# A hybrid diffusion layer on one core: hand-written engine and load orders up to the end of the q projection

## The chip, the cores and the metric

The kernel runs on one core of a Trainium2 chip. The metric is the device time in microseconds of one execution. The core has five instruction streams that matter here: PE (matrix products; PEld is its loading of weights), DVE (vector operations), ACT (scalar and activation operations), POOL (a second vector engine) and SP (which only issues transfers). Each stream runs its own instructions in order and waits on semaphores for the others. Matrix products accumulate in PSUM, eight banks, and their results are copied out by DVE or ACT.

## The reference, cut to what matters

One layer for 640 tokens: 512 latent tokens (four tiles of 128) and 128 context tokens (the fifth tile, number 4). The width is 1024.

```python
def _layer(x, cond, rope, ctx_k, ctx_v, ...):
    mod = (jax.nn.silu(cond) @ w_ada + b_ada)[:, None, :]
    sh1, sc1, g1, sh2, sc2, g2 = jnp.split(mod, 6, axis=-1)
    h = _rms(x, norm_mix) * (1 + sc1) + sh1
    mix, k, v = _mixer(h, rope, ctx_k, ctx_v, ...)      # proj = h @ w_in: q, k, v, conv inputs
    x = x + g1 * mix
    h2 = _rms(x, norm_ffn) * (1 + sc2) + sh2
    gate, up = jnp.split(h2 @ w_gate_up, 2, axis=-1)
    x = x + g2 * ((jax.nn.silu(gate) * up) @ w_down)
    return x, k, v
```

Inside the mixer, `q = _rms(q, q_norm)` and the same for k are followed by the rotary positions on latent tokens, attention, a gated short convolution, and an output projection. Everything is float32. The part of the kernel that is changed computes `h` and `h @ w_in[:, :512]`, the q projection, and the tables of cosines and sines times the norms' gains.

## The kernel before, in words

A product of two float32 matrices is made of three products in a faster format (float32r): each operand is split into a rounded high part and a low part, the difference, and `mm3` adds high x high, high x low and low x high. `split` makes the two parts, the high one on ACT (L150), the low one on DVE (L151).

The start works in eight rounds k, one for each 128 rows of the model's width. Before the rounds each of the five tiles of x is loaded, its squares are summed on ACT (L476), its scale is made by DVE and POOL (`rstd_of`, L162 and L164), it is scaled by DVE (L478), turned by PE in eight transposes (L439), and copied from PSUM to `xT` by DVE or ACT (L450, L452). For every k:

- `ada1_mm(k)`, the step "a": a block of `w_ada` of 1 MB, loaded in two halves of two transfers each into a ring `af` of four halves, is multiplied by the condition in 16 products (L379); DVE copies the result (L421).
- `ada1_mod(k)`, the step "m": four small products turn that result (L428); DVE makes scale and shift of block k from it (`mod_evict`, L402 to L406).
- `h_do(k, ...)`, the step "h": the modulated tile, on ACT for the latent tokens (L462) and on DVE for the context (L464), then the split into `hH[k]` and `hL[k]`.
- `q_mm(k, t)`, the step "q" for each token tile t: three products of 512 columns (L154 to L156) into the accumulator of the tile. The weights of q come as four transfers, each for two rounds; a transfer lands in a ring `wf` of three buffers and is split into rings `wh`, `wl` of four.

The order of the work is set in this way. A string of steps, `P1PRE`, is written out for the first round and the work before it; in it the orders of DVE, ACT and POOL are kept as written. The other seven rounds follow the pattern `P1SEQ`, in which only PE's order is kept as written: m and h for block k+1, a for block k+2, then five q products. A planner orders the other engines there from costs and priorities. SP's transfers are ordered by the planner all the way; `LOADS` gives only the order in which the first of them are asked for. Weights are asked for a few places ahead of their use (`W`, `AHEAD`): the two transfers of the k and v weights and the first of the convolution's are asked for within the rounds.

PSUM has two banks of kind t, two of kind c and two pairs of kind s at this stage. The turned tiles 0 to 2 use the pairs, tiles 3 and 4 and the m products use t, the a products use c. The q accumulators take both pairs and one of c when the first q product comes.

At the end of q the five accumulators are copied out (L549, L551). Then the rotary tables are made: two transfers on ACT's queue (L561, L562) and ten POOL operations (L568, L574). Products for k and v follow (PE names them `pc`, 256 columns), then attention, which PE runs from a third written string, `SEQ`.

Of the kernel before, what the change touches and what calls it, by code (L numbers as in the profile page):

```python
# [86 lines left out]
LOADS = [0, 0, 0, 0, 2, 1, -1, 0, 3, 3, 2, 2]  # L87
# [3 lines left out]
def build(ctx, tc, x_prompt, x_sample, c, cache_k, cache_v, c_ctx, norm_mix, norm_ffn, w_ada, b_ada,  # L91
# [144 lines left out]
    def load_split(e, wf):  # L236
# [4 lines left out]
        if gain is None:  # L241
            with early(SOQ[key[1]] if key[0] == 'q' else SOW):
# [109 lines left out]

    for a in LOADS:
        if a > 0:
            ada1_next(a)
        elif a < 0:
            load_next(True)
        else:
            x_load()
# [53 lines left out]
    def ada1_mm(k):  # L413
# [3 lines left out]
        for h, wf in enumerate(ada1[k]):  # L417
            for i in range(4):
                cond_mm(rp, 4 * h + i, wf[:, i].rearrange("p a b -> p (a b)"))
        res = T("res", (P, 256), F32, 2)  # L420
        dve.tensor_copy(res, rp)  # L421
        ada1[k] = res

    def ada1_mod(k):
        res = ada1.pop(k)
        mp = PB((P, 2, 1, 2))
# [5 lines left out]

    def xT_do(t):

        both = PS2() if t < XB else None
        tps = [both[:, i] if t < XB else PB() for i in range(2)]

        def turn(k):
            pe.transpose(tps[k // 4][:, k % 4 * P:(k % 4 + 1) * P], xs[t][:, k * P:(k + 1) * P], ident)  # L439

        if t < XB:
            for k in range(KD):
                turn(k)
        for i, tp in enumerate(tps):
            if t >= XB:
                for k in range(4):
                    turn(4 * i + k)
            dst, src = xT[:, 4 * i:4 * i + 4, t * P:(t + 1) * P], tp.rearrange("p (k q) -> p k q", q=P)
            if XTE[2 * t + i] == 0:
                act.activation(dst, src, AF.Copy)  # L450
            else:
                dve.tensor_copy(dst, src)  # L452
# [3 lines left out]
    def h_do(k, cc):  # L456
# [3 lines left out]
        a, b = modA[0][:, k, cc:cc + 1], modB[0][:, k, cc:cc + 1]  # L460
        if cc == 0:
# [3 lines left out]
        if k == 0:  # L465
# [3 lines left out]

    pe_order = tc.manual_schedule(engines={mybir.EngineType.PE})  # L470
    pe_order.__enter__()

    def x_norm(t):
# [3 lines left out]
        r = rstd_of(ss, 1, 1.0 / D)  # L477
        dve.tensor_scalar_mul(xs[t], xs[t], r)  # L478
# [9 lines left out]
    qacc = []  # L488

    def q_mm(k, t):  # L490
        if not qacc:
            qa, qb = PS2(), PS2()
            qacc.extend([qa[:, 0], qa[:, 1], qb[:, 0], qb[:, 1], PB(tag="c")])
        wh, wl = W(("q", k // 2))
        s = slice(t * P, (t + 1) * P)
        mm3(qacc[t], hH[k][:, s], hL[k][:, s], wh[:, k % 2], wl[:, k % 2], k == 0, k == KD - 1)
# [15 lines left out]
    steps = {"r": x_norm, "c": late_consts, "w": lambda i: load_split(*deferred.pop(0)), "p": lambda i: rows2_load(), "x": xT_do, "v": lambda i: (vec_do, vec2_do)[i](), "m": ada1_mod, "a": ada1_mm}  # L512
    pre_order = tc.manual_schedule(engines={mybir.EngineType.DVE, mybir.EngineType.Activation, mybir.EngineType.Pool})
    pre_order.__enter__()
    in_pre[0] = True
    for x in P1PRE.split():
        k = int(x[1])
        if x[0] == "h":
            h_do(k, int(x[2]))
        elif x[0] == "q":  # L520
            q_mm(k, int(x[2]))
        else:
# [7 lines left out]
    for k in range(1, KD):  # L530
        ada1_next(3)
        for x in P1SEQ.split():
            if x == "m" and k + 1 < KD:
                ada1_mod(k + 1)
            elif x == "h" and k + 1 < KD:
                h_do(k + 1, 0)
                h_do(k + 1, 1)
            elif x == "a" and k + 2 < KD:
                ada1_mm(k + 2)
            elif x.isdigit():  # L540
                q_mm(k, int(x))
        if k == 2:
            vec2_do()

# [18 lines left out]
    gains, tabs = [], []  # L563
    for nm, g in (("q", q_norm), ("k", k_norm)):
        gb_ = gain_rows[nm]
        tab = T("tab", (P, 2, NL, HD), F32, 2)
        cg, sg = tab[:, 0], tab[:, 1]
        pool.tensor_tensor(cg, rc, gb_.unsqueeze(1).to_broadcast([P, NL, HD]), ALU.mult)  # L568
        s4 = sg.rearrange("p t (a b c) -> p t a b c", a=2, b=2)
        r4 = rs_.rearrange("p t (a b c) -> p t a b c", a=2, b=2)  # L570
        g4 = gb_.rearrange("p (a b c) -> p a b c", a=2, b=2)
        for b in range(2):
            for a in range(2):
                pool.tensor_tensor(s4[:, :, a, b], r4[:, :, a, b],  # L574
                                   g4[:, a, 1 - b].unsqueeze(1).to_broadcast([P, NL, 16]), ALU.mult)
        gains.append(gb_)
# [747 lines left out]
```

## Time and profile before

| | |
|---|---|
| median of 3 runs | 760.62 us (759.63 to 762.23) |
| the profiled execution: time | 762.66 us |
| the profiled execution: span of the core | 760.9 us |
| PE busy over the span | 739.5 us (97%) |
| DVE, ACT, POOL busy over the span | 552.7, 369.6, 43.1 us |
| first product behind q (k and v) | starts at 64.82 us |
| mean granted clock of PE | 0.993 |

The profile is of one execution and its times count from the start of the span. The span is a little shorter than the execution's time. PE's share of busy time is high throughout, but a busy PE is not PE at its peak, since its clock can be cut to half. The profile gives the granted clock for any stretch (1.00 is full). In a row of the timeline the first number is the start, the second the length, and the bracket behind it the idle time of the engine before the instruction and what ended it.

### The profile page before, as it was taken

How to read it: one execution, taken by the hardware profiler on the slowest of the kernel's cores; microseconds unless marked ns; L12 is line 12 of the kernel's file. 1: busy time of each engine (PE TensorE's matmuls, PEld its weight loads, DVE VectorE, ACT ScalarE, POOL GpSimd, SP SyncE). 2: the span in 40 equal slices, each digit the busy share in tenths (PEclk: the TensorE clock that was granted, in tenths of full speed). 3: DMA queues.
4: the chain of work that ended last, by engine and by line, in shares of the span. 5: the costliest groups of instructions: out<-in, count | busy, mean ns of one | idle time of the engine just before them, and what ended most of it. 6: DMA issues, size and time to landing. Idle time of an engine off the chain costs nothing.

```text
span 760.9 us, 11844 instructions
## 1 busy us (share of the span) xinstructions
PE 739.5 (97%) x4580; PEld 664.6 (87%) x4580; DVE 552.7 (73%) x1003; ACT 369.6 (49%) x715; POOL 43.1 (6%) x73
## 2 busy tenths in 40 slices
PE   4999999999999999999999999999999999999997
PEld 3768888989998887899898789998889998899986
DVE  5556987676666797779879678884578866788653
ACT  5345867666656444765552135553125541255410
POOL 3104301011010110100000000000000000000000
PEclk9899999999999999999999999999999999999999
DMA  9985132522433363031335223223113132222312
GB/s 289 293 233 158 38 118 91 173 91 91 160 104 93 130 249 111 1 112 56 86 111 179 83 62 103 79 89 113 53 56 110 58 112 67 73 86 82 111 56 84
DMA packets 102349, 84.52 MB, mean 111 GB/s; under 512 B 4526, under 2 KB 82674, under 8 KB 102292
## 3 DMA queue, kind: packets, MB, share of 16 engines
q1 hardware_dynamic: 100980, 83.39, 35.5%
q8 instruction: 36, 0.59, 0.3%
q10 hardware_dynamic: 1056, 0.26, 0.2%
q0 software_dynamic: 256, 0.11, 0.1%
q14 instruction: 21, 0.17, 0.1%
HBM read 79.68 MB, written 2.75 MB: 108 GB/s over the span
## 4 chain that ended last, share of the span: by engine, by line
PE 82%; DVE 8%; DMA 3%; ACT 2%; SPq 2%; issue 1%; POOL 1%; DVEq 0%; POOLq 0%
PE pf L154 17%; PE pf L156 16%; PE pf L155 16%; PE pc L677 3%; PE pc L678 3%; PE pc L679 3%; PE po L834 3%; PE ps L791 2%; PE ph L154 2%; PE pt L817 2%; PE ph L155 2%; PE ph L156 2%; PE pc L379 2%; DMA af<-in_w_ada_dram 2%; DMA wf<-in_w_gate_up_dram 1%
## 5 line engine op out<-in xcount | busy, mean ns | idle before, releaser
L150 ACT ACTIVATE wh<-wf 128x1024 fp32r<-128x1024 f32 (+1 forms) x76 | 64.1, 843 | 95.7 <-PE pf L156 61.8
L154 PE MATMUL pf<-wh,gT 128*128 128x512 f32 (+1 forms) x225 | 88.1, 392 | 0.0
L155 PE MATMUL pf<-wl,gT 128*128 128x512 f32 (+1 forms) x225 | 87.7, 390 | 0.0
L156 PE MATMUL pf<-wh,gT 128*128 128x512 f32 (+1 forms) x225 | 87.7, 390 | 0.0
L151 DVE TENSOR_TENSOR wl<-wf,wh 128x1024 fp32r<-128x1024 f32 (+1 forms) x42 | 49.4, 1175 | 29.1 <-ACT wh L150 26.3
L677 PE MATMUL pc<-hH,wh 128*128 128x320 f32 x192 | 61.1, 318 | 0.0
L678 PE MATMUL pc<-hL,wh 128*128 128x320 f32 x192 | 59.4, 310 | 0.0
L679 PE MATMUL pc<-hH,wl 128*128 128x320 f32 x192 | 59.4, 309 | 0.0
L155 PEld LDWEIGHTS pf<-wl,gT 128*128 128x128 f32 x225 | 42.2, 188 | 10.0 <-issue 0.2
L154 PEld LDWEIGHTS pf<-wh,gT 128*128 128x128 f32 x225 | 42.2, 188 | 9.9 <-ACT wh L150 0.2
L156 PEld LDWEIGHTS pf<-wh,gT 128*128 128x128 f32 x225 | 42.2, 188 | 9.8
L154 PE MATMUL pf<-T,wh 128*128 128x320 f32 x160 | 49.7, 311 | 0.5 <-ACT u L1154 0.5
L155 PE MATMUL pf<-T,wl 128*128 128x320 f32 x160 | 49.5, 309 | 0.0
L155 PE MATMUL pf<-T,wh 128*128 128x320 f32 x160 | 49.5, 309 | 0.0
L156 PE MATMUL pf<-T,wh 128*128 128x320 f32 x160 | 49.5, 309 | 0.0
L154 PE MATMUL pf<-T,wl 128*128 128x320 f32 x160 | 49.5, 309 | 0.0
L156 PE MATMUL pf<-T,wl 128*128 128x320 f32 x160 | 49.5, 309 | 0.0
L154 PE MATMUL pf<-B,wl 128*128 128x320 f32 x152 | 47.3, 311 | 0.1
L156 PE MATMUL pf<-B,wl 128*128 128x320 f32 x152 | 47.1, 310 | 0.0
L155 PE MATMUL pf<-B,wl 128*128 128x320 f32 x152 | 47.0, 309 | 0.0
L1233 DVE TENSOR_TENSOR dm<-pf,g 128x512 f32<-128x512 f32 (+1 forms) x41 | 27.7, 675 | 22.8 <-PE pf L156 22.6
L154 PE MATMUL pf<-B,wh 128*128 128x320 f32 x136 | 42.3, 311 | 1.5 <-DVE cu L1183 1.5
(293 smaller groups left out, 2023.9 us busy)
## 6 DMA issues: line engine op xcount, KB each, us to landing
wf<-in_w_gate_up_dram SPq DMA_DIRECT2D x44, 512.0 KB, 4.0
aw<-in_w_ada_dram SPq DMA_DIRECT2D x24, 512.0 KB, 4.7
wf<-in_w_down_dram SPq DMA_DIRECT2D x20, 512.0 KB, 3.4
wf<-in_w_in_dram SPq DMA_DIRECT2D x18, 512.0 KB, 6.1
af<-in_w_ada_dram SPq DMA_DIRECT2D x32, 256.0 KB, 6.0
x<-in_x_sample_dram SPq DMA_DIRECT2D x8, 512.0 KB, 4.8
wf<-in_w_out_dram SPq DMA_DIRECT2D x8, 512.0 KB, 3.9
wf<-in_w_ada_dram SPq DMA_DIRECT2D x8, 512.0 KB, 3.7
```

The costliest lines, as they stand in the source:

```text
L150: act.activation(hi, src, AF.Copy)
L151: dve.tensor_tensor(lo, src, f32(hi), ALU.subtract)
L154: pe.matmul(out, lh, rh, start=start, stop=False, skip_group_check=more)
L155: pe.matmul(out, lh, rl, start=False, stop=False, skip_group_check=more)
L156: pe.matmul(out, ll, rh, start=False, stop=stop, skip_group_check=more)
L379: pe.matmul(out[CG * g:CG * (g + 1)], cp[:, k], w, start=(k < 4), stop=(k >= KD - 4), skip_group_check=True)
L677: pe.matmul(acc, wh[:, k], hH[k][:, c0:c0 + n], start=(k == 0), stop=False)
L678: pe.matmul(acc, wh[:, k], hL[k][:, c0:c0 + n], start=False, stop=False)
L679: pe.matmul(acc, wl[:, k], hH[k][:, c0:c0 + n], start=False, stop=(k == KD - 1))
L791: pe.matmul(s2[:, g, :320], q, kk[:, v, P + g * 320:P + (g + 1) * 320], start=(i == 0), stop=(i == 1))
L834: pe.matmul(ov, w, x[:, i].rearrange("p a q -> p (a q)"), start=(g == 0 and i == 0 and n == 0), stop=(last and i == len(kts) - 1 and n == 1))
L1233: dve.tensor_tensor(dm, ps[:, :n], g2[cc][:, oc], ALU.mult)
```

## The change

It replaces the order of everything up to the end of q. One string, `P1SEQ`, now names every step of the start and of all eight rounds, and the orders of PE, DVE, ACT, POOL and SP are all kept as it is written. The steps are cut finer: scaling a tile ("s") apart from its norm ("r"), each copy of a turned tile ("e", with the engine, d for DVE and a for ACT) apart from its turning ("x"), the copy of an a product ("b") apart from the product, and the two halves of a weight split ("w" on ACT, "l" on DVE) apart. New steps are "d", a number of small products on the identity that go to the fifth accumulator before it is used, "n", the low part of the first modulated tile, and "R", the rotary tables.

- In the rounds, a of block k+2 stands behind two q products of round k instead of ahead of all five; m and h of block k+1 stand at the end of the round before.
- The loads: `LOADS` gives the whole order: all tiles of x, blocks 0 to 7 with q0, q1 and q2 between them, and then q3, the two transfers of k and v weights, and the first of the convolution's. The transfers of the caches come behind that list.
- The first modulated tile (block 0, latent tokens; the step `h00y`): ACT writes the rounded `hH[0]` straight from `xT`, DVE makes the unrounded one beside it, and "n" takes the difference. Before, ACT made the unrounded one, then the rounded one from it.
- Both copies of turned tiles 0 and 1 are DVE's; before, one of each was ACT's.
- The rotary tables are made in round four, from transfers on POOL's queue, in a buffer that is otherwise used late.
- The fifth q accumulator is taken at the start, so the a products and the first two m products share one bank of kind c.

```diff
-SOQ = [0, -300, -300, -300]
-P1SEQ = 'm h a 0 1 2 3 4'
-P1PRE = ('r0 r1 r2 x0 r3 x1 v0 x2 a0 w0 x3 m0 r4 h00 a1 q02 q01 x4 q00 m1 h01 h10 a2 q03 h11 p0 q04 c0')
+P1SEQ = ('d8 r0 s0 x0 r1 s1 r2 e00d x1 s2 e01d r3 v0 d4 x2 s3 e20a a0 e10d b0 e11d e21d x3 m0 d4 w e30a h00y l n0 '
+         'r4 q01 e31d s4 p0 q02 a1 x4 b1 e40d m1 h01x h10 q00 a2 b2 h11 q04 m2 w e41a q03 l q10 h20 q11 q12 h21 a3 b3 q13 q14 '
+         'm3 h30 h31 q20 q21 a4 b4 q22 q23 c0 q24 v1 m4 h40 h41 R q30 q31 a5 b5 w l q32 q33 q34 '
+         'm5 h50 h51 q40 q41 a6 b6 q42 q43 q44 m6 h60 h61 q50 q51 a7 b7 w l q52 q53 q54 '
+         'm7 h70 h71 q60 q61 w l q62 q63 q64 w l w l q70 q71 q72 q73 q74')
-XTE = [0, 1, 0, 1, 1, 1, 0, 1, 1, 0]
-LOADS = [0, 0, 0, 0, 2, 1, -1, 0, 3, 3, 2, 2]
+LOADS = 'xxxxAWxAAWAAWAAAWWWW'
...
+    pe_order = tc.manual_schedule(engines={mybir.EngineType.PE})
+    pe_order.__enter__()
+    pre_order = tc.manual_schedule(engines={mybir.EngineType.DVE, mybir.EngineType.Activation, mybir.EngineType.Pool,
+                                            mybir.EngineType.SP})
+    pre_order.__enter__()
...
-        mp = PB((P, 2, 1, 2))
+        mp = PB((P, 2, 1, 2), tag="c" if k < 2 else "t")
...
+        if alone and cc == 0:
+            act.activation(hH[k][:, s], xT[:, k, s], AF.Identity, bias=b, scale=a)
+            dve.tensor_scalar(hF[k][:, s], xT[:, k, s], a, b, ALU.mult, ALU.add)
+            return
...
-    qacc = []
+    qacc = [PB(tag="c")]
...
+    def spin(n):
+        for _ in range(n):
+            pe.matmul(qacc[-1][:, :P], ident, ident, start=True, stop=True)
...
+    def w_hi(_):
+        e, wf = deferred.pop(0)
+        a, b = e[1].shape[1], e[1].shape[2]
+        e[5] = T("wh", (P, a, b), F32R, WHB), T("wl", (P, a, b), F32R, WHB)
+        act.activation(e[5][0], wf, AF.Copy)
+        rounded.append((wf, *e[5]))
...
+    def rope_tables():
+        rt = T("oz", (P, 2, NL, HD))
+        rc, rs_ = rt[:, 0], rt[:, 1]
+        pool.dma_start(rc, rope_c.rearrange("(t p) d -> p t d", p=P))
+        pool.dma_start(rs_, rope_s.rearrange("(t p) d -> p t d", p=P))
...
-    for k in range(1, KD):
-        ada1_next(3)
-        for x in P1SEQ.split():
...
-    rt = T("pr", (P, 2, NL, HD), F32, PRB)
-    rc, rs_ = rt[:, 0], rt[:, 1]
-    act.dma_start(rc, rope_c.rearrange("(t p) d -> p t d", p=P))
-    act.dma_start(rs_, rope_s.rearrange("(t p) d -> p t d", p=P))
```

More of the change, by code (lines that the diff above doesn't have):

```diff
@@ L241, in load_split @@
         if gain is None:
[L242 removed]
+            with early(SOW):
                 split(wh, wl, wf)
@@ L556, in build @@
     open_psum("pp2", {"t": PT, "c": 5 - PT, "o": 1, "s": 1})
-    rt = T("pr", (P, 2, NL, HD), F32, PRB)
-    rc, rs_ = rt[:, 0], rt[:, 1]
-    act.dma_start(rc, rope_c.rearrange("(t p) d -> p t d", p=P))
-    act.dma_start(rs_, rope_s.rearrange("(t p) d -> p t d", p=P))
[L563 to L576, printed above, removed]
-        tabs.append((cg, sg))
     def head_norm(ps, nh, t, which):
```

103 lines of the change are left out of this document (58 added, 45 removed).

## The prediction

> **What bounds the kernel now.** I read the page first, for the clock, then a table of busy time cut where the clock changes, then the timeline of the stretch that the change touches. The page says where to look:
>
> ```profile
> span 760.9 us, 11844 instructions
> PEclk9899999999999999999999999999999999999999
> ```
>
> The profiled execution took 762.66 us, 1.76 more than its span and 2.04 more than the median of 760.62; the sum below is made inside its span and its difference is then taken from the median. After the first tenth the clock never leaves 9, and PE is the bound there. Everything edited lies ahead of the end of q. That start, cut at the clock's changes (columns: stretch, PE, PEld, DVE, ACT, POOL busy, granted clock, DMA share, GB/s):
>
> ```profile
> 14.66:18.07 3.41, 1.18 (x14) 0.71 (x12) 3.07 (x9) 2.57 (x5) 0.23 (x1) 1.00 1.15 298
> 18.07:21.49 3.42, 2.33 (x15) 1.07 (x12) 1.87 (x3) 1.18 (x2) 3.31 (x6) 0.50 1.17 290
> 21.49:24.90 3.41, 3.41 (x14) 2.91 (x13) 0.62 (x1) 0.00 (x0) 0.00 (x0) 0.50 1.16 282
> 24.90:38.56 13.66, 13.66 (x100) 9.98 (x99) 7.70 (x25) 6.50 (x10) 0.00 (x0) 1.00 1.02 297
> 38.56:41.97 3.41, 1.89 (x22) 1.00 (x21) 2.52 (x6) 2.73 (x3) 0.00 (x0) 1.00 1.01 269
> 41.97:45.38 3.41, 3.41 (x14) 2.48 (x8) 1.65 (x4) 1.32 (x2) 0.00 (x0) 0.50 1.09 307
> 45.38:64.82 19.44, 19.44 (x113) 15.13 (x112) 9.05 (x21) 7.25 (x10) 1.42 (x2) 1.00 0.74 207
> ```
>
> The half-clock stretches are 6.83 and 3.41 us long, and each follows 3.41 us in which PE worked 1.18 or 1.89: the clock is judged about every 3.4 us by the share of busy time. DMA is full until 45, and PE has no idle time in 24.90 to 38.56 or from 41.97 on. So the start is bound in turn by loads, by the idle PE's halved clock, and by PE. The PE rows that carry it (start, length, and in brackets the idle time before):
>
> ```profile
> 15.98 0.61 PE L428 MATMUL pt<-sel,res 128*128 128x2 f32 x4 [1.17 <-ACT xT L450]
> 17.64 0.72 PE L379 MATMUL pc<-af,cp 128*32 128x256 f32 x8 [1.06 <-DMA af<-in_w_ada_dram]
> 19.45 1.08 PE L379 MATMUL pc<-af,cp 128*32 128x256 f32 x8 [1.09 <-DMA af<-in_w_ada_dram]
> 29.96 0.50 PE L154 MATMUL ps<-wh,hH 128*128 128x512 f32 x1
> 41.57 0.75 PE L379 MATMUL pc<-af,cp 128*32 128x256 f32 x8 [1.52 <-DMA af<-in_w_ada_dram]
> 52.74 1.07 PE L379 MATMUL pc<-af,cp 128*32 128x256 f32 x16
> 53.74 0.50 PE L154 MATMUL ps<-wh,hH 128*128 128x512 f32 x1
> 57.35 0.50 PE L428 MATMUL pt<-sel,res 128*128 128x2 f32 x4
> 57.71 0.48 PE L154 MATMUL ps<-wh,hH 128*128 128x512 f32 x1
> 64.82 0.28 PE L154 MATMUL pc<-wh,hH 128*128 128x256 f32 x1
> ```
>
> q of round one begins at 29.96, and q ends at 64.82, where the k and v product starts. Between starts, a modulation product (a) costs 53.74 - 52.74 = 1.00, a q round 57.35 - 53.74 = 3.61, an m 0.36. Two stalls stand out: three waits of 1.06 to 1.17 before 19.45, and one of 1.52 before 41.57.
>
> **The change, part by part.** *The order of the loads.* These are SP's issues before:
>
> ```profile
> 30.71 1.31 SPq L224 DMA_DIRECT2D wf<-in_w_in_dram  x2
> 32.12 4.97 SPq L323 DMA_DIRECT2D af<-in_w_ada_dram  x4
> 37.19 2.48 SPq L224 DMA_DIRECT2D wf<-in_w_in_dram  x1
> 39.76 5.62 SPq L323 DMA_DIRECT2D af<-in_w_ada_dram  x6
> 2.00:28.00 26.00, 17.08 (x111) 12.48 (x112) 13.27 (x36) 11.85 (x22) 7.03 (x13) 0.87 1.07 313
> 28.00:48.00 20.00, 18.48 (x121) 13.36 (x124) 10.53 (x29) 9.41 (x11) 0.00 (x0) 0.91 1.03 288
> ```
>
> The half block that PE awaited at 41.57 was issued behind two q weights (30.71). Changed, q3 and the kv weights stand behind all modulation blocks. By 28.00 some 313 x 26 = 8.14 MB have come, which covers the five x tiles (2.62), blocks 0 to 3 (4.19), q0 and q1 (1.05) and the small rows (0.13). At 288 GB/s block 4 (1.05 MB) then ends near 31, q2 (0.52) near 33, and blocks 5, 6, 7 near 36.6, 40.3 and 43.9. The semaphore comes later than the bytes: before, the awaited half stood at 11.2 MB (x, blocks 0 to 5, four q weights, caches and rows), that is 38.6 by this sum, and came at 41.57; the second half of block 1 stood at 5.3 MB, 18.9 by 313 GB/s, and came at 19.45. So I add 0.5 to 3 us. PE will want blocks 3 to 7 near 29.5, 34, 39, 44 and 49 (worked out below), since each a now stands behind two q products; block 3 (bytes near 27.5) is the only one close. I take the stall as gone: 1.52 saved, and the halved clock after it (3.41 at 0.50 is 1.7 of work; I count 1.6). If the later bound of the lag holds, block 3 costs up to 1.5.
>
> Wait that is added: DVE's b (the copy of a product) stands in a written order, so a late block holds the weight splits and h tiles queued behind it. They are used a round later, about 5 us, which covers it; without the cover q waits as long as the block. Blocks k+2 still wait for a of block k, as before, since the ring is unchanged.
>
> *The first round and the spins.* The rows they are made from (the last is four f32 products of 512 columns):
>
> ```profile
> 9.87 0.60 ACT L450 ACTIVATE xT<-ps 128x512 f32<-128x512 f32 x1 [0.57 <-PE ps L439]
> 10.19 0.75 DVE L478 TENSOR_SCALAR x<-x,rs 128x1024 f32<-128x1024 f32 x1 [0.66 <-POOL rs L164]
> 10.86 0.68 DVE L452 COPY xT<-ps 128x512 f32<-128x512 f32 x1
> 11.60 1.09 PE L439 MATMUL ps<-ident,x 128*128 128x128 f32 x8
> 12.62 1.16 PE L379 MATMUL pc<-af,cp 128*32 128x256 f32 x16
> 15.56 1.22 DVE L151 TENSOR_TENSOR wl<-wf,wh 128x1024 fp32r<-128x1024 f32 x1
> 17.29 0.15 DVE L402 TENSOR_TENSOR modt<-pt,vec 128x2 f32<-128x2 f32 x1
> 17.80 0.81 ACT L462 ACTIVATE hF<-xT,modB,modA 128x512 f32<-128x512 f32 x1 [0.84 <-DVE ms L162]
> 18.65 0.63 ACT L150 ACTIVATE hH<-hF 128x512 fp32r<-128x512 f32 x1
> 19.31 0.69 DVE L151 TENSOR_TENSOR hL<-hF,hH 128x512 fp32r<-128x512 f32 x1
> 20.59 0.42 DVE L421 COPY res<-pc 128x256 f32<-128x256 f32 x1 [0.59 <-PE pc L379]
> 26.47 0.34 DVE L464 TENSOR_SCALAR hF<-xT,modA,modB 128x128 f32<-128x128 f32 x1
> 129.62 1.72 PE pc L739 x4
> ```
>
> The spins, sixteen small products on the identity: 1.72 / 16 is 0.11 for 128 columns, 0.22 cold, so the first eight take 0.9 to 1.8 while x0 is still being loaded and scaled, and four take 0.4 to 0.9 in each of two gaps. Cost 0; at worst 0.5 where x2 is ready sooner than worked out here. They hold the fifth accumulator from the start, so a1 must wait for m0's eviction (done long before its data) and a2 for m1's.
>
> x0's two copies are now both DVE's, with a scaling between: 9.87 + 0.68 + 0.75 + 0.68 is 12.0, so x2 starts near 12.1 instead of 11.60 and a0 near 13.2 instead of 12.62: 0.5 lost. But m0's eviction now comes behind three copies and b only: b0 (0.42) ends near 14.7, e11 and e21 near 16.1, so the eviction (three operations like the one of 0.15, some 0.5) runs at 16.1 to 16.6 where it began at 17.29. Rounding directly, hH of tile 0 is there 0.81 later (17.5; before it took 0.81 + 0.63 and ended at 19.3). The low part gains less: DVE's own scale and add (128x512; between 0.34 and 0.75, I take 0.45), the weight's low part (1.22) and the difference (0.69) give 19.0 against 20.0. So two q products run in the gap before block 1's second half (19.45) and end near 20.0 at full clock. Then a1 ends at 21.0, x4 (1.09) at 22.1, its copy 0.68 and m1's eviction end at 23.4; h01 and h10 (0.34, then 0.81 on ACT) at 24.9; then 0.34 on DVE, a rounding on ACT and a difference, each 128x640 (0.7 to 0.8 by the 128x512 rows), end at 26.9. PE meanwhile does q00, a2, q04, m2, q03 and can begin q10 near 26.4.
>
> But the clock: between 14.66 and 18.07 PE now does half of x3 (0.6), m0 (0.4), four spins (0.4 to 0.5) and one q product (0.2), about 1.7 of 3.41, less than the 1.89 that cost the clock at 41.97. So 18.07 to 21.49 is slow again; after 18.8 PE is then kept busy, and I take the second slow stretch (21.49 to 24.90) as gone. That delays q10 by about 1.0, to 27.4. The Trainium skill, "TensorE: Matmul & The Clock Gate", section on HAM oscillation, asks only that no gap exceed about 3.4 us. Here a gap of 1.52 was enough, so the trace disagrees; by the rule q10 would stay at 26.4.
>
> *Tables, cache loads, splits.* One POOL row and the DVE row behind it:
>
> ```profile
> 66.36 2.15 POOL L574 TENSOR_TENSOR tab<-pr,gnk 128x64 f32<-128x64 f32 x4
> 68.23 0.28 DVE L586 TENSOR_REDUCE hq_ss<-ph 128x2 f32<-128x128 f32 x1 [0.75 <-ACT ph L584]
> ```
>
> The rotary tables' ten POOL operations and two loads leave the end of q for round four, where POOL has nothing; loads go from ACT's queue to POOL's, behind the five gain rows that are there already. Before, POOL ended them at 68.51 and DVE's first user waited for ACT, not for POOL: gain 0, at most the 0.75 shown. Without the move they would now be late, so it keeps the gain rather than makes one. The caches' loads go behind SP's written list, whose last entry waits for q3's split, which stands behind a7 (49) in the order, near 51; with the lag above they land ahead of 57, before q ends. The late constants and the second row of vectors move inside the start and are first used behind q: 0. The split of conv0's weights stays ahead of q's last round, covered by q. From q's end the same PE order follows, moved as a whole: 0, between -0.7 and +1.5, since another order on DVE and ACT behind q could cost a wait.
>
> **Sum.** Round one starts 29.96 - 27.4 = 2.56 sooner, less a3 (1.00), which before stood ahead of it; plus the stall 1.52; plus the clock 1.6: 4.7. q ends near 60.1 and the run takes 760.62 - 4.7 = 755.9 us. With the bounds (block 3 up to 1.5 late, -0.7 to +1.5 behind q, the start 0.7 either way, and not every loss at once) this case spans 754.5 to 758.1.
>
> **Rivals.** *No slow clock at the start* (0.24): the spins and q01 lift the busy share enough; 4.7 + 1.0, so 754.9. This is what the rule of the Trainium skill's page on TensorE named above would give. For it: 1.7 against 1.89 is a near thing. Against it: 2.33 of 3.42 in slow state did not bring the clock back.
>
> *The order does not bring the blocks sooner* (0.09): the ring, not the weights, held them back, and one stall with its slow stretch stays: 4.7 - 1.52 - 1.6 = 1.6 gained, 759.0. For it: DMA is full whatever the order. Against: 0.52 MB fewer stand ahead of block 5.
>
> *Nothing is carried past q* (0.07): attention's start waits for something that did not move, the cache loads or a new order on DVE; the 4.7 is given back, 760.6. Against: before, PE still worked without a break at 64.82.
>
> *Starved rounds, slower* (0.07): a3 to a7 each wait, since each is released to load block k+2 later than before; every stall costs 1.52 and its slow stretch 1.6. From two stalls the gain is gone; with three the run is 3 x 3.1 - 4.7 = 4.6 slower, 765.2. It decides once blocks 4 to 7 and q2 (4.7 MB in the 19.5 us from 29.5 to 49) come at under 241 GB/s. Against: 288 was seen.
>
> **How the numbers follow.** The forecast has 0.53. A measurement can tell about 0.3%, 2.3 us, from no change. Forecast and warm start are faster (0.77), the next two the same (0.16), starvation slower (0.07). The range 752.5 to 759.5 takes in the first three cases: at its low end the warm start with 1.4 of gains from the bounds and 1.0 for the spread of runs (759.63 to 762.23 before), at its high end the third case. It leaves out the last two.
>
> **What would show it.** Right: q's end near 60; no idle PE above 0.7 us after q10; q10 near 27; one half-clock stretch ahead of 25 and none near 42; hH of tile 0 ending near 17.5; tables done by 50. Wrong: PE idle in front of L379 in several rounds (starved), an unchanged first use of round one (the first round's chain misjudged), or q ending at 60 with the later PE rows not moved (nothing carried).

## The result: slower by 0.3%, and the profile after

| | before | after |
|---|---|---|
| median | 760.38 us (759.62 to 762.23, 14 runs) | 762.75 us (761.23 to 764.56, 14 runs) |
| ratio after to before | | 1.003, 95% interval 1.0021 to 1.0039 |
| profiled execution: time, span | 762.66, 760.9 us | 763.84, 762.1 us |
| first k and v product (q's end) | 64.82 us | 63.09 us |
| from there to the first score product of attention | 12.61 us | 14.91 us |

The changed kernel is slower, by about 2.4 us. In its profiled execution q ends 1.73 us sooner, but the stretch behind q is 2.30 longer. The timeline of PE of the changed kernel (start, length, and in brackets the idle time before and what ended it; a0, the first modulation product, is the first row):

```profile
12.73 1.07 PE L385 MATMUL pc<-af,cp 128*32 128x256 f32 x16
15.03 1.14 PE L507 MATMUL pc<-ident 128*128 128x128 f32 x8
16.83 0.50 PE L155 MATMUL ps<-wh,hH 128*128 128x512 f32 x1 [0.67 <-ACT hH L470]
25.55 0.39 PE L155 MATMUL ps<-wh,hH 128*128 128x512 f32 x1
28.25 0.64 PE L385 MATMUL pc<-af,cp 128*32 128x256 f32 x8 [0.19 <-issue]
31.25 1.08 PE L385 MATMUL pc<-af,cp 128*32 128x256 f32 x8 [2.37 <-DMA af<-in_w_ada_dram]
63.09 0.28 PE L155 MATMUL pc<-wh,hH 128*128 128x256 f32 x1
70.58 0.37 PE L647 MATMUL pt<-identr,osq 128*128 128x128 f32 x2 [1.64 <-ACT osq L639]
```

The first q product runs at 16.83 and round one (q10) begins at 25.55, 4.41 ahead of the 29.96 of before and 1.85 ahead of the forecast. Then two waits stand out: 2.37 us for the second half of block 3, where the forecast allowed up to 1.5, and 1.64 behind q, for ACT, where it has nothing. The table of busy time, cut at these places (columns as in the prediction):

```profile
17.00:24.77 7.77, 7.31 (x60) 4.45 (x61) 5.56 (x14) 2.09 (x5) 5.08 (x8) 1.00 1.14 305
24.77:28.25 3.48, 3.29 (x15) 2.11 (x14) 2.52 (x6) 2.95 (x5) 0.00 (x0) 1.00 1.15 269
28.25:31.25 3.00, 0.64 (x8) 0.18 (x9) 0.82 (x1) 0.41 (x1) 1.82 (x5) 0.96 1.17 288
31.25:34.66 3.41, 3.41 (x14) 2.18 (x15) 0.42 (x1) 0.00 (x0) 2.05 (x6) 0.53 1.04 301
34.66:63.09 28.43, 28.43 (x178) 20.60 (x176) 15.85 (x39) 14.24 (x20) 0.00 (x0) 1.00 0.75 226
69.00:78.00 9.00, 6.18 (x41) 5.90 (x41) 6.79 (x26) 4.98 (x15) 3.46 (x4) 0.81 0.25 72
```

The granted clock is full (1.00) up to 31. Each of the two waits is followed by about 3.4 us at half clock: 0.53 in 31.25 to 34.66, and 0.81 in the mean of 69 to 78. Between 34.66 and 63.09 PE is busy all the time. What held block 3 back is seen in the issues, SP's first and then POOL's, of the same execution:

```profile
18.18 0.83 SPq L225 DMA_DIRECT2D wf<-in_w_in_dram  x1
19.05 0.47 SPq L589 DMA_DIRECT2D ck<-in_cache_k_dram  x1
19.57 0.43 SPq L591 DMA_DIRECT2D cv<-in_cache_v_dram  x1
20.13 9.74 SPq L324 DMA_DIRECT2D af<-in_w_ada_dram  x8
...
21.91 0.79 POOL L555 DMA_DIRECT2D oz<-rope_c_dram  x1
22.69 0.78 POOL L556 DMA_DIRECT2D oz<-rope_s_dram  x1
```

The caches are asked for at 19.05, not behind SP's list: their two issues (L589, L591) stand behind the end of the written part, and the planner put them ahead of block 3. The rotary tables' transfers go out at 21.91, not in round four: POOL's queue had nothing to wait for. Together 0.39 MB stand ahead of or beside block 3 where the DMA engines are full (share 1.14 to 1.17 above). And q1, the issue at 18.18, stands ahead of block 3 as well, 0.52 MB more. In the kernel before it was the other way round. These are SP's issues there; the first row ends with the four transfers of block 3, and the last is q1:

```profile
17.29 4.55 SPq L323 DMA_DIRECT2D af<-in_w_ada_dram  x5
21.89 0.83 SPq L527 DMA_DIRECT2D ck<-in_cache_k_dram  x1
22.77 0.43 SPq L529 DMA_DIRECT2D cv<-in_cache_v_dram  x1
23.24 0.43 SPq L224 DMA_DIRECT2D wf<-in_w_in_dram  x1
```

The chain of waits of the changed kernel has both losses (start, length, what):

```profile
22.05 9.07 DMA af<-in_w_ada_dram
...
58.14 1.05 ACT wh L526
59.21 1.24 DVE wl L533
60.47 4.98 DMA wf<-in_w_in_dram
65.53 1.07 ACT wh L151
```

The last transfer of block 3 took 9.07 us from issue to landing. Behind q the chain is another one: ACT and DVE split the k and v weights only at 58.14 and 59.21, behind m7 and h7 in the written order. That frees the buffer for the convolution's second load at 60.47, which lands near 65.5. Its split then stands on ACT in front of the k norm (L610) for which PE waits.

### The profile page after: what moved, and what is told of

Read it like the earlier page. It is cut to its first block, busy times and chain, and to the rows that moved or that the text cites. A ratio compares the mean times of both kernels' runs of the same rounds, so it can differ in the third digit from the quotient of the medians.

```text
span 762.1 us, 11916 instructions
## 1 busy us (share of the span) xinstructions
PE 742.6 (97%) x4612; PEld 666.7 (87%) x4612; DVE 553.9 (73%) x1005; ACT 368.0 (48%) x713; POOL 43.8 (6%) x75
## 4 chain that ended last, share of the span: by engine, by line
PE 84%; DVE 6%; DMA 5%; ACT 2%; issue 1%; SPq 0%; POOL 0%; DVEq 0%; ACTq 0%
PE pf L157 17%; PE pf L156 17%; PE pf L155 17%; PE pc L703 3%; PE pc L705 3%; PE pc L704 3%; PE po L860 2%; PE ps L817 2%; PE pc L385 2%; PE ph L155 2%; PE ph L157 2%; PE ph L156 2%; PE pt L843 2%; DMA af<-in_w_ada_dram 2%; DMA es<-t 1%
## 5 line engine op out<-in xcount | busy, mean ns | idle before, releaser
L151 ACT ACTIVATE wh<-wf 128x512 fp32r<-128x512 f32 (+1 forms) x69 | 56.6, 821 | 85.6 <-PE pf L157 62.0
L152 DVE TENSOR_TENSOR wl<-wf,wh 128x1024 fp32r<-128x1024 f32 (+1 forms) x35 | 40.6, 1161 | 28.7 <-ACT wh L151 23.6
```

The source lines that it names most:

```text
L151: act.activation(hi, src, AF.Copy)
L152: dve.tensor_tensor(lo, src, f32(hi), ALU.subtract)
```

## The experiments

Behind each ratio is its 95% interval. q's end is the start of the first k and v product in the profile. "Behind" is the time from there to the first score product, and "half clock" how long the granted clock was 0.5 in the profiled execution. It comes in stretches of 3.4 us, and the place of each stands with it. Before and after, as profiled above, had 10.2 (three stretches) and 6.8. A profile shows one execution, which can lie off the median of its kernel: that of splits_early took 759.66 us, that of small_late 759.46 and that of before_spins 763.91.

| kernel | median us | ratio to before | q's end | behind | half clock |
|---|---|---|---|---|---|
| before_again | 760.67 (1 run) | | 61.32 | 13.03 | 6.8 (20, 74) |
| before_third | 759.16 (1 run) | | 61.56 | 12.62 | 3.4 (19) |
| after_again | 762.55 | 1.0026 (1.0013 to 1.004) | 61.69 | 13.53 | 0 |
| after_third | 761.85 (1 run) | | 61.20 | 13.56 | 6.8 (10, 75) |
| spins_out | 762.35 | 1.0022 (1.001 to 1.0035) | 61.37 | 15.25 | 6.8 (20, 71) |
| first_tile_undone | 762.09 | 1.0026 (1.0011 to 1.0041) | 60.83 | 14.84 | 3.4 (70) |
| tables_late | 761.71 | 1.0008 (0.9995 to 1.0022) | 60.55 | 14.96 | 3.4 (69) |
| small_late | 760.82 | 1.001 (0.9996 to 1.0023) | 60.17 | 13.68 | 0 |
| block3_first | 762.98 | 1.004 (1.0024 to 1.0056) | 62.54 | 13.38 | 3.4 (10) |
| splits_early | 762.2 | 1.0024 (1.0009 to 1.0039) | 60.83 | 12.61 | 3.4 (9) |
| two | 760.63 | 1.0002 (0.9989 to 1.0016) | 59.86 | 12.61 | 3.4 (72) |
| three | 760.04 | 0.9997 (0.9985 to 1.001) | 60.80 | 12.61 | 0 |
| two_a_first | 759.79 | 0.9986 (0.9977 to 0.9996) | 59.66 | 12.61 | 0 |
| before_spins | 761.51 | 1.0019 (1.0006 to 1.0031) | 61.59 | 16.49 | 6.8 (69) |
| before_tables | 762.7 | 1.0027 (1.0012 to 1.0041) | 63.23 | 12.68 | 3.4 (21) |
| spins_tables | 762.57 | 1.0028 (1.0015 to 1.0041) | 62.57 | 12.67 | 6.8 (9) |
| tables_at_22 | 761.39 | 1.0017 (1.0003 to 1.003) | 63.55 | 12.67 | 3.4 (19) |
| spins_tables_at_22 | 762.3 | 1.0036 (1.0021 to 1.005) | 62.61 | 12.68 | 0 |

**Was the execution that the prediction costed an ordinary one?** before_again and before_third are the kernel before, once more each.

> The kernel before, profiled once more. Theory A (the prediction took one slow execution for the rule: 762.66 against a median of 760.4): q ends 1.5 to 2.5 us ahead of 64.8, because the wait of 1.52 on block 5 or a half-clock stretch is shorter or absent, and the stretch from q's end to the context scores (12.6 us) stays. Theory B (the profiled execution is typical): q ends within 0.5 us of 64.8 with the same two stalls.

> The kernel before once more, for its profile. If the profiled execution of the prediction (q's end 64.82, a wait of 1.52 on block 5 and a half-clock stretch at 42) was a rare one, q ends at 61 to 62 here, the waits after 25 are below 0.7 and no half clock lies between 25 and 60. If it was an ordinary one, q ends at 64 to 65 with that wait.

PE's rows of before_third:

```profile
29.07 0.50 PE L154 MATMUL ps<-wh,hH 128*128 128x512 f32 x1
39.78 0.64 PE L379 MATMUL pc<-af,cp 128*32 128x256 f32 x8 [0.62 <-DMA af<-in_w_ada_dram]
61.56 0.28 PE L154 MATMUL pc<-wh,hH 128*128 128x256 f32 x1
67.80 0.36 PE L621 MATMUL pt<-identr,osq 128*128 128x128 f32 x2 [0.38 <-ACT osq L613]
```

It was not. Block 5 was awaited for 0.62 here and 0.56 in before_again, not 1.52; no half clock follows it, and q ends at 61.3 to 61.6, not at 64.82. Among 28 runs of before the mean granted clock was 0.9958, and only 4 had the 0.993 of the costed execution or less.

**Do the two losses of the change recur?** after_again and after_third are the changed kernel.

> The changed kernel, profiled once more and timed beside the variants. Theory A (the loss is behind q): from q's end to the first context scores it takes 14 to 15 us again, against 12.6 before, with PE idle 1.2 to 2.2 us ahead of the first turned keys; q's end moves between runs with block 3's landing (60 to 63). Theory B (the loss is in the start): the stretch behind q is 12.6 to 13 in this profile and q ends later than 62.5. The time is 762.0 to 763.5 beside variants of 762.2 (splits earlier) and 760.8 (small transfers later).

> The changed kernel once more, for its profile. Theory (two losses that belong to its order): PE waits 1.3 to 2.4 for the second half of block 3 near 30, 1.3 to 2.2 for ACT behind q, and the stretch from q's end to the scores takes 13.5 to 15.3 where 12.6 is had with the splits early. Rival (the losses are chance of the executions seen): one of the two waits is below 0.6.

Block 3 was awaited for 1.38 and 0.33 (2.37 at first), and the wait for ACT behind q was 1.31 and 1.33 (1.64 at first). So the wait behind q recurs, and the one on block 3 varies: where the start itself was later (a0 at 14.57 in after_third, 12.73 at first), block 3 is nearly in time. q10 began at 26.79 and 27.35, against 28.87 and 29.07 in the two further executions of before.

**Parts undone.** spins_out takes the three groups of small products out of the changed kernel.

```diff
-P1SEQ = ('d8 r0 s0 x0 ... v0 d4 x2 ... m0 d4 w ...
+P1SEQ = ('r0 s0 x0 ... v0 x2 ... m0 w ...
```

> The changed kernel without its sixteen spins. Theory A (the spins keep the clock up): in the changed kernel no stretch ahead of 31 us is at half clock and q of round one starts at 24.8. Without the spins x0 and x1 are turned at half clock (0.22 a transpose instead of 0.14), 18 to 21.5 us is at half clock, and q10 starts 1 to 2.5 us later; but block 3 lands at the same 31.3, so q ends within 0.5 us of 63.1 and the time stays within 0.1%. Theory B (the early start comes from the written order alone): q10 stays within 0.5 of 24.8. Theory C (the spins are worth time to the end): the run is 1 to 2 us slower.

The ratio is 1.0022, within the interval of after. The half clock came back in the first round (20 to 24), a1 began at 20.50 (19.43 in after), and block 3 was no longer awaited: what the start lost was time in which the loads caught up. q10 began at 28.08, and q still ended at 61.37. The clock is the spins' doing: in all six profiles of kernels without them a stretch at half clock begins between 18 and 22, and in none of the 14 with them does one begin between 11 and 31 (in four of those it comes earlier, near 10).

first_tile_undone lets ACT write the unrounded first tile and round it from there, as before.

```diff
-            act.activation(hH[k][:, s], xT[:, k, s], AF.Identity, bias=b, scale=a)
-            dve.tensor_scalar(hF[k][:, s], xT[:, k, s], a, b, ALU.mult, ALU.add)
+            act.activation(hF[k][:, s], xT[:, k, s], AF.Identity, bias=b, scale=a)
+            act.activation(hH[k][:, s], hF[k][:, s], AF.Copy)
```

> The changed kernel with the first modulated tile made as before: ACT writes the unrounded tile and then the rounded one from it. Theory A (it shortens one link of a chain that then waits for block 1 and block 3): hH of that tile comes 0.6 us later, q01 starts 0.6 later, block 3 lands at the same time, the time stays within 0.5 us of 762.6. Theory B (the link is on the path to q's end): the time is 0.6 us or more above.

PE then waits 1.28 for the first tile instead of about 0.65, and block 3 is not awaited at all. The ratio stays: the direct rounding shortens this wait, and nothing of it is left in the time. That it is given back at block 3 is argued only, since block 3 was nearly in time in after_third too, where a0 was as late.

tables_late puts the tables' two transfers on SP behind block 7; small_late puts the two cache transfers there as well.

```diff
-LOADS = 'xxxxAWxAAWAAWAAAWWWW'
+LOADS = 'xxxxAWxAAWAAWAAATWWWW'   # T: rope_c, rope_s (small_late: and the caches), on SP
-        pool.dma_start(rc, ...)
-        pool.dma_start(rs_, ...)
```

> The changed kernel with the rotary tables' two transfers alone (0.26 MB) on SP's queue behind block 7. Theory A (they land beside block 3 since POOL's queue waits for nothing ahead of them, and delay it by 0.26 MB / 0.293 = 0.9 us): the wait on block 3 shrinks by about 0.9, the time is 0.7 to 1.5 us below the changed kernel's 762.6. Theory B (the caches were the larger part): the time stays within 0.4 of 762.6.

> The changed kernel with the transfers of the rotary tables (0.26 MB) and of the caches (0.13 MB) issued on SP's queue behind modulation block 7 instead of beside block 3. Theory A (block 3's second half comes late by the bytes ahead of it): it lands 0.39 MB / 0.293 = 1.3 us sooner, near 29.9, the wait of 2.4 on PE shrinks to about 1.1 and q ends 1 to 1.5 sooner (more where the half-clock stretch behind it goes too: up to 3). Theory B (the ring or the issue holds block 3 back): the wait stays within 0.3 of 2.4. Either way the stall behind q is unchanged, since conv weights still come late.

Both go down, to 1.0008 and 1.001. In small_late block 3 is not awaited and q ends at 60.17; the wait behind q (1.45) stays. So by the medians the transfers' place was worth 1 to 2 us. The intervals don't tell the two kernels apart, and they overlap with that of after_again.

block3_first asks for block 3 ahead of q1 and moves q1's split to the end of round one.

```diff
-... 'm2 w e41a q03 l q10 h20 q11 q12 h21 a3 b3 q13 q14 '   LOADS = 'xxxxAWxAAWAAWAAAWWWW'
+... 'm2 e41a q03 q10 h20 q11 q12 h21 a3 b3 q13 q14 w l '   LOADS = 'xxxxAWxAAAWAWAAAWWWW'
```

> The changed kernel with block 3 asked for ahead of q1, and q1's split moved behind q14. Theory A (bytes ahead): block 3's second half lands 0.52 MB / 0.293 = 1.8 us sooner, near 29.5, q ends 1.5 to 3.5 us sooner, if q1 (then landing near 31) is split before q20 wants it. Theory B (ring or issue): the wait on PE stays at 2.4 and q ends where it did or later. A gain at q's end is cut behind q if conv1's weights still land near 65.5: then the time moves by less than 0.5 us.

The wait on block 3 is down to 0.50, but the next step waits 0.75 for q1's split, and the ratio is 1.004. So here the order only chose which load was late.

splits_early moves one of the two late splits ahead of m7.

```diff
-... q52 q53 q54 ' 'm7 h70 h71 q60 q61 w l q62 q63 q64 w l w l q70 ...
+... q52 q53 q54 w l ' 'm7 h70 h71 q60 q61 w l q62 q63 q64 w l q70 ...
```

> The changed kernel with the split of the first k and v weights written ahead of m7 instead of behind q61, the later ones one place earlier each. Theory A (the stall behind q comes from conv1's weights, whose buffer is freed by that split, and whose own split stands on ACT ahead of the k norm): conv1 lands 2 to 4 us sooner, the 1.64 us of idle PE at 70.6 falls to 0.4 as before, the half-clock stretch of 72 to 75.3 goes, and the run is 2 to 3 us faster (760). Theory B (the stall comes from the norm chain itself now that q ends sooner): the idle PE stays at 1.2 or more and the time stays within 0.5 us.

ACT's rows of splits_early, then PE's row behind q:

```profile
61.03 1.06 ACT L151 ACTIVATE wh<-wf 128x1024 fp32r<-128x1024 f32 x1 [1.65 <-PE pc L157]
62.00 2.04 ACT L598 ACTIVATE of<-ps 128x512 f32<-128x512 f32 x4
...
67.06 0.36 PE L647 MATMUL pt<-identr,osq 128*128 128x128 f32 x2 [0.39 <-ACT osq L639]
```

The convolution's split now runs at 61.03, ahead of q's copies, where it began at 65.53 in after. PE's wait is 0.39, and the stretch behind q is 12.61, as before. All four kernels with this split moved have 12.61, and all eight profiles of the changed kernel without it, parts undone or not, have 13.38 to 15.25. That the late splits lengthen the stretch is shown: by 0.9 us without half clock (after_again), and by 2.3 with it (after). The time does not follow: 2 to 3 us were expected, and the ratio is 1.0024. The profile is of an execution 2.5 us below its median, and what the others lose is not seen.

**Parts put together.** two is small_late and splits_early, three adds block3_first, and two_a_first is two with a5, a6 and a7 directly behind m, ahead of the q products.

```diff
-... m4 h40 h41 R q30 q31 a5 b5 w l q32 q33 q34 ' 'm5 h50 h51 q40 q41 a6 b6 q42 ...
+... m4 a5 h40 h41 b5 R w l q30 q31 q32 q33 q34 ' 'm5 a6 h50 h51 b6 q40 q41 q42 ...
```

> The changed kernel with two edits: transfers of tables and caches behind block 7, and the split of the first k and v weights ahead of m7; block 3 stays behind q1. Theory A (the variant with three edits drew its 760.0 from these two, since block 3 ahead of q1 alone gave nothing): 759.3 to 760.6, no wait on PE above 0.8 us between 24 and q's end, 12.6 us from there to the context scores. Theory B (block 3's place is needed too): a wait of 0.5 to 1.5 on block 3 stays and the time is 760.5 to 762.

> The changed kernel with three edits together: transfers of tables and caches behind block 7, block 3 ahead of q1, the split of the first k and v weights ahead of m7. Theory A (the gain of the start is real, and is lost to block 3's lateness and to the late splits): no wait on PE above 0.8 us between 24 and the end of q, q ends near 59.5 to 60.5, 12.6 us from there to the context scores, and the time is 757.0 to 759.0, faster than before by 0.2 to 0.4%. Theory B (nothing but the order of the first round counts, and it costs as much as it gives): the time stays at 760.5 to 762.

> The two edits, and the modulation products of blocks 5 to 7 put directly behind m again, as before the change, instead of behind two q products. Theory A (each product between q's costs 0.1 to 0.2 us at its borders, and blocks 5 to 7 land in time): a round falls from 5.14 to about 5.0 us, q ends 0.3 to 0.5 sooner, the time moves 0 to 0.5 us down. Theory B (the place behind two q products is what hides the blocks): PE waits 0.5 us or more on blocks 5, 6 or 7 and the time is 0.5 to 2 us up.

All three have 12.61 behind q, and two and three are level with before; for three 757.0 to 759.0 had been expected. The scores begin at 72.47 in two and at 73.41 in three, where the two further executions of before have 74.18 and 74.35. So the start's gain reaches the scores, and is lost behind them; where, the next experiments show. two_a_first is the only kernel faster than before, by 0.14%. Its rows: q10, block 3, q's end and the wait behind q.

```profile
25.88 0.40 PE L155 MATMUL ps<-wh,hH 128*128 128x512 f32 x1
29.44 0.64 PE L393 MATMUL pc<-af,cp 128*32 128x256 f32 x8 [0.49 <-DMA af<-in_w_ada_dram]
59.66 0.28 PE L155 MATMUL pc<-wh,hH 128*128 128x256 f32 x1
65.89 0.37 PE L648 MATMUL pt<-identr,osq 128*128 128x128 f32 x2 [0.39 <-ACT osq L640]
```

That it beats two is not settled, since the intervals overlap. Its q ends only 0.20 sooner, and from q10 to q's end PE is busy for 33.29 us, against 33.31 in two: the place of a5 to a7 gained nothing there.

**One part alone, in the kernel before.** before_spins has only the spins.

```diff
-P1PRE = ('r0 r1 r2 x0 r3 x1 v0 x2 a0 w0 x3 m0 r4 ...
+P1PRE = ('d8 r0 r1 r2 x0 r3 x1 v0 d4 x2 a0 w0 x3 m0 d4 r4 ...
```

> The kernel before with the sixteen spins alone (eight ahead of x0, four behind the vector turn, four behind m0), into the fifth accumulator, which is taken at the start as in the changed kernel. Theory A (the spins lift the clock, and PE's time at the start is on the path): no half-clock stretch ahead of 25, q of round one 1 to 2.5 us sooner, the run 0.5 to 2 us faster than before. Theory B (the start waits for loads, whatever the clock): q's rounds start sooner but wait for blocks 3 to 5 longer, and the time stays within 0.5 us.

It is slower, by 0.19%. Its rows of ACT's queue, of POOL and of PE around the end of q:

```profile
56.83 1.34 ACTq L566 DMA_DIRECT2D pr<-rope_s_dram  x1
65.18 1.16 POOL L578 TENSOR_TENSOR tab<-pr,gnq 128x64 f32<-128x64 f32 x4 [4.46 <-DMA pr<-rope_s_dram]
66.30 1.17 POOL L578 TENSOR_TENSOR tab<-pr,gnk 128x64 f32<-128x64 f32 x4
...
69.73 1.09 PE L625 MATMUL pt<-identr,osq 128*128 128x128 f32 x4 [2.28 <-ACT osq L617]
```

The rotary tables, still made behind q, end at 67.47, and the k norm waits for them: 2.28 of PE, and 6.8 us at half clock with it. But q did not end sooner here (61.59, against 61.56 in before_third). What was late is the tables' second transfer: asked for at 56.83 by an issue of 1.34, it let POOL start at 65.18, where before_third has 56.80, 0.52 and 62.22. Then the tables alone. In before_tables the planner put their transfers at 7.40 and 8.52, ahead of a norm that then runs at 9.31 (8.29 in before_third), and a0 began at 14.66 (12.62 to 13.69 in the three profiles of before), so this run doesn't price the place that the change gives them. tables_at_22 does.

```diff
+        pool.dma_start(rt[:, 0], rope_c...)    # behind conv_w, at 21.89
+        pool.dma_start(rt[:, 1], rope_s...)
...
         if k == 2:
             vec2_do()
+        if k == 4:
+            rope_tables()                      # before_tables: with its transfers
```

> The kernel before, with one part of the change alone: the rotary tables made in round four, their two transfers on POOL's queue. Theory (the transfers are asked for as soon as POOL's queue comes to them, about 22, and take the bandwidth from a block of the modulation weights; the tables were not on the path behind q in an ordinary execution): the first block loaded after 22 lands up to 1 us later, the stretch from q's end to the scores stays at 12.6 to 13.0, and the median is 0 to 1 above that of before, ratio 1.000 to 1.001. Rival (the late tables cost the kernel before a wait behind q as well): the stretch falls below 12.6 and the ratio is 0.998 to 0.999.

> The kernel before with the rotary tables in round four and their two transfers on POOL's queue behind the five small rows, so asked for at about 22, as in the changed kernel. In the run with the tables moved the planner put these transfers at 7.40 and 8.52, ahead of a norm. Theory (0.26 MB more among the blocks' loads at 22 costs what it takes to move, 0.9 at 290 GB/s, on the block that PE waits for; the start is untouched): the first modulation product starts at 13 to 14 as before, the wait on block 5 or block 3 grows to 0.6 to 1.5, and the ratio is 1.000 to 1.0015. Rival (the place is free, and the whole loss of 1.0027 came from the norm that waited): ratio 0.998 to 0.9995, no wait above 0.6.

In tables_at_22 block 5 is awaited for 1.27, block 4 for 0.63, and q ends at 63.55. The three profiles of before have 0.56, 0.62 and 1.52 for block 5, so the wait alone proves nothing; the ratio does. The tables at the place of the change cost the kernel before 0.17%, some 1.3 us. The rival of a free place is out. Then both with the spins:

> The kernel before with the spins and with the rotary tables of round four. Theory (the spins alone were 0.9 to 1.2 slower because q ended sooner in clock terms and the tables were then late by 2.3 behind q): with the tables early the gap behind q goes (0.4 to 0.8 instead of 2.28), no half clock follows q, and the ratio falls from 1.0019 to 0.999 to 1.0005. Rival (the spins cost by themselves, by holding a bank and by delaying the first transposes): the ratio stays near 1.002.

> The same with the spins. Theory (the loss of the spins alone was the late tables): a gap behind q below 0.6, and a ratio not above that of the same kernel without spins. Rival (the spins cost by themselves): no such gap, and the ratio 0.001 or more above that kernel's.

The gap behind q is 0.45 in both, so the late tables had made the 2.28. But the times did not follow. With its cover the spins should have gained; they are level with the kernel without them in the one pair (1.0028 and 1.0027) and 0.0019 slower in the other (1.0036 and 1.0017, with intervals that overlap). So the theory that the late tables were all of the spins' loss falls. One place is seen in the profiles. SP's, DVE's and PE's rows of spins_tables_at_22, in attention:

```profile
217.53 1.77 SPq L857 DMA_DIRECT2D es<-t  x1
...
223.09 0.42 DVE L863 TENSOR_TENSOR of<-t,es 64x256 f32<-64x256 f32 x1 [2.22 <-DMA es<-t]
...
225.85 0.61 PE L911 MATMUL pt<-ones,osq 128*128 128x1 f32 x4 [0.95 <-ACT osq L865]
```

And of tables_at_22, the same transfer and operation:

```profile
218.57 0.60 SPq L853 DMA_DIRECT2D es<-t  x1
...
223.02 0.42 DVE L859 TENSOR_TENSOR of<-t,es 64x256 f32<-64x256 f32 x1 [1.10 <-DMA es<-t]
```

The kernel with spins comes to this place 1.04 sooner and loses it here: one issue of a 64 KB transfer takes 1.77 instead of 0.60, and PE waits 0.95, where it has no wait in tables_at_22. It recurs. PE waits at this product (`pt<-ones,osq`) in all 14 profiles of kernels with spins, for 0.30 to 1.09 (0.51, 0.64 and 0.30 in the three of the changed kernel), and in none of the six without, spins_out among them. From the first score product to the end of the span the kernels without spins take 683.2 to 683.8 us and those with them 683.8 to 684.9, 0.9 more in the mean (three profiles with a half clock behind the scores left out). And for the stretch from 214 to 222 the profile's list of DMA queues has a row like this one (queue, kind, packets, MB, share) in all 14, and in none of the six:

```profile
q8 instruction: 1, 0.02, 1.5%
```

The sixteen spins move the moment at which a packet of instructions is loaded, from behind these transfers to beside them. In before_spins such a packet also falls in 56 to 58, beside the tables' late transfer, and in before_third none does. That the packet makes the issue and the landing late is argued from this coincidence; no run moves it by itself.

## Why the prediction was wrong

*The stall of 1.52 and the half clock of 1.6* are the step that failed first. They are 3.1 of the 4.7 forecast, and they belong to one execution. The prediction says that this execution took 2.04 more than the median, and then takes the 4.7 from the median all the same. In two other executions the wait was 0.56 and 0.62, with no half clock after it. From an ordinary 61.4, the forecast end of q at 60.1 is a gain of 1.3, not of 4.7.

*The first round* was mis-sized the other way, by its clock. The prediction has q10 at 27.4 with one slow stretch, and at 26.4 without; the runs have 25.55, 26.79 and 27.35, the first with the earliest a0, and none has a stretch at half clock between 14 and 31. That is the mechanism of the warm start, there a rival. The spins do it: without them (spins_out) the clock is halved from 20 on. They take longer than was worked out (four took 1.14 at full clock, recorded as eight products, where 0.4 to 0.9 stood), but they stand in idle time. The first tile's rounded part ended near 16.8 in the first execution, sooner than the 17.5 forecast; in the others it came with the later a0 (near 18.0 and 18.6).

*The order of the loads* failed at block 3. The prediction saw that block 3 was the close one, and allowed up to 1.5. Its sum of bytes has q1 with block 3, which in the kernel before stood ahead of q1, but it has not the caches, which it put behind SP's list, nor the tables, which it put in round four; they were issued at 19.05 and 21.91. A step's place in the written order tells when an engine comes to it, and POOL, with nothing to wait for, came to it about 20 us before round four. By the prediction's bytes and lag block 3 was due at 28.0 to 30.5; PE could start on its second half at 31.25, 31.23 and 30.76. In the first execution PE moreover came to the block 1.3 us sooner than forecast (28.25 against 29.5). tables_at_22 prices this in the kernel before (0.17%), small_late in the changed one (from 1.0026 to 1.003 down to 1.001, with intervals that overlap). The later blocks were in time, as forecast, and the rival of starved rounds is out.

*Behind q* the prediction has 0, between -0.7 and +1.5: "the same PE order follows, moved as a whole". The stretch took 13.53 to 14.91 where before takes 12.61 to 13.03. The splits that the written order moves were costed at nothing, with q as cover. What was not followed is the buffer that a split frees, the transfer that waits for it, and that transfer's split ahead of the norm on ACT. splits_early shows it.

*The tables' gain* was called cover: 0, but without the move they would be late. Late tables did cost 2.28 in before_spins, though not because q ended sooner. And the 0 was read from one execution: in before_again DVE waited for the tables, and PE 0.80 where it has 0.38 in before_third. That POOL "has nothing" in round four held, but the DMA engines were full where the transfers went out.

*Behind the scores* the prediction has no term at all. The spins were priced by PE's time at the start alone, "Cost 0; at worst 0.5". PE waits 0.30 to 0.64 in attention in the three profiles of the changed kernel, and not at all in those of before and of spins_out.

So the sum comes out as: a round one that begins 1.5 to 3.5 us sooner than in the two ordinary executions of before. Of this the a that now stands inside it takes 1.0, and the same products take PE some 0.6 longer (33.52 us busy from q10 to q's end in after_third, 31.87 and no such a in before_third; why is open). Block 3 takes 0.3 to 2.4 and its half clock up to 1.7, so that q ends at 61.2 to 63.1, where before ends it at 61.3 to 61.6. Then 0.5 to 2.3 are lost behind q, and more behind the scores. Taken whole, after_again is 2.5 us longer than before_third: 0.13 of it up to q's end, 0.91 behind q, and 1.5 from the scores to the end. The likeliest rival by its result was the one in which nothing is carried past q; the measured time lies 2.2 above it, since time was lost as well as not gained.

The Trainium skill, "TensorE: Matmul & The Clock Gate", section on HAM oscillation, was cited for gaps up to about 3.4 us being harmless. Here gaps of 2.37 and 1.64 were each followed by some 3.4 us at half clock, while a gap of 1.38 (after_again) was not; the measurement decides against the rule. What goes with the half clock here is the busy share of a window: PE worked 1.10 and 1.53 of the 3.41 us ahead of the two stretches of after, and 2.34 ahead of that of two, where the longest gap was 0.69. The windows keep a beat as well: the starts of the two stretches of after lie 12 times 3.41 us apart, and those of before_again 16 times. So the same gap may cost nothing or 1.7 us: three has the gaps of two behind q, and no half clock there.

## What to carry to other kernels

Before costing a stall from a profile, set that execution against the spread of runs: where it is 2 us slow, its stalls are the first suspects, and a second profile costs little. Compare the stages to the end of the span and not the edited one alone: of the 2.5 us above, 1.5 lay 15 us and more behind the edit. When a start is made faster, ask which load each step will then find missing, and list every small transfer that has no wait in front of it, since it can be issued long before the place where it is written (21.91 here instead of round four) and then takes its share of full DMA engines. When a split is moved, follow the buffer that it frees to the next load, and that load's own split to the engine on which it will stand ahead of something urgent.

## What the runs showed of the hardware

- Small transfers on POOL's queue take bandwidth from SP's large ones. In after, the last transfer of block 3 was 9.07 us from issue to landing, with 0.39 MB of small transfers about it; the median of such transfers is 6.7 in after and 6.0 in before. The Trainium skill, "DMA: Bandwidth & Descriptors", section "Issuing engines are not separate DMA queues", says that transfers interleave on the same engines whoever starts them; the trace agrees.
- The start of a0 moves between executions of one kernel by up to 1.8 us (12.73, 14.00 and 14.57 in after), so a gain there needs several profiles to be seen.
- One issue of a 64 KB transfer on SP in attention, near 214 to 221, took 0.90 to 1.94 instead of 0.60 in 11 of the 14 profiles of kernels with spins, and in none of the 6 without. In all 14 a packet of instructions is loaded between 214 and 222 and PE waits 0.30 to 1.09 there; in the 6 neither happens. So sixteen small products at the start cost time some 200 us later. That the packet is the reason is not shown.
